# Two chunks in flight in a recurrence, and sample pages spread over a whole attention layer

## Chip, cores, metric

One Trainium2 chip, all eight cores, one launch. Each core runs the same program on its own share: a prompt of 2048 tokens and four sample sequences of four tokens. The metric is device microseconds (us) of the slowest core, from its first to its last instruction. A chip has two dies, cores 0 to 3 and cores 4 to 7.

How runs are compared needs a word, because it decides what the numbers below mean. Three things make cores differ here. (1) In some executions cores of one die run dense matmuls at a lower granted clock. (2) Even in undisturbed runs one die of a chip is slower than the other, by 25 to 90 us; on the chip of the two main profiles that is die 1, on two other chips die 0. (3) Now and then a pair of cores of the slower die is slower still. A run is labelled slow when one die is over 1% longer at a lower clock. Experiments often met a disturbed die, so I compare *medians of the four cores of one undisturbed die*: the faster die of one kernel with the faster die of another, the slower with the slower.

## Reference, cut to what matters

```python
# layer 0: eight units per token tile, four HGRN2 and four retention, each a chunked recurrence
def step(S, inp):                       # one chunk
    A = einsum(q, k) * rel              # masked decay inside the chunk
    o = einsum(A, v) + einsum(q * exp(G), S)     # inside + carried state
    S = S * exp(G_end) + einsum(k_dec, v)        # state for the next chunk
# layer 1: differential attention, 4 heads, two key maps each
#   prompt: causal softmax over 2048 tokens
#   sample: softmax over 8192 past tokens from a paged cache
k_past = cache_k[page_table]            # 64 pages of 128 tokens per sequence, in random order
v_past = cache_v[page_table]
```

Each core handles 4 x 64 = 256 pages; one page holds the keys (or values) of all four heads, 128 x 1024 elements.

## The kernel before

Every operation is put on an engine's queue by a helper, which also works out the semaphore waits: an operation waits for the last writer of what it reads, and for all readers of what it overwrites. The helper guards PSUM by bank (`P0` to `P7`). In the timeline the page work of TensorE comes in the order of the queue (transposes at 2706.68, scores at 2707.53, values at 2709.19 us on core 1, after 1.26 us of waiting, and the next prompt scores only at 2709.52), so what matters is which wait stands in front of what.

Layer 0, one unit and tile (cut): four or six projections, then the chunks one after another.

```python
def proj(ws_ap_fn, t0, n, pi, rkeys):   # pi: PSUM bank, 0, 1, 2, 0, 1, 2 ... by hand; norm in P3
    for c in range(NCH): matmul(P[pi], ...)
...
for ci in range(nchunks):
    matmul(P[4], kTt, qTt)                        # scores inside the chunk
    transpose(Pb[6], kTt); transpose(Pb[6], vTt)
    dve: Am = P[4] * mask                         # ONE Am, kvtok, qd
    act: kvtok = copy(P[6])
    matmul(P[7], kvtok_v, Am)
    matmul(P[7], Sbf, q_in)                       # carried state
    matmul(P[5], kvtok_k, kvtok_v)
    dve: U = U * decay + P[5]                     # state, float32
    dve or act: Sbf = U * ...                     # state, bf16, for the next chunk
```

Layer 1, the sample pages: a generator, one step per call, each step working on three pages.

```python
for sstep in range(NP + 2):                       # NP = 256
    stageA(sstep)       # 8 transposes of the K page into P0, copy to SBUF (DVE or ACT in turn)
    stageB(sstep - 1)   # 8 score matmuls into P1, exponential on ACT -> PTs
    stageC(sstep - 2)   # 8 value matmuls into P1 with PTs, DVE adds P1 to acc
    kdma(sstep + 2); vdma(sstep + 1)              # indirect gather of later pages
    yield
...
for h in range(4):
    load_head_weights(h); project(...)            # dense
    for each query tile, key map, key block:
        scores(kbi + 1); values(kbi)
        next(gen)                                 # one page after EVERY key block
    for each output-projection point:
        ...; next(gen)
```

## Time and profile before

The kernel took 4996.0 us (median of 20 runs on the chip of the comparison, fastest 4982.7). The phases of two cores, cut at the first matmul of each phase in the trace, in us (core 1 stands for the faster die, core 5 for the slower one):

| phase | core 1 | core 5 |
|---|---|---|
| layer 0, recurrent units | 1177 | 1171 |
| attention of heads 0, 1, 2, 3 | 382, 387, 249, 146 | 398, 400, 250, 146 |
| output projections | 117, 130, 30, 30 | 119, 129, 30, 30 |
| projections (first with the samples') | 149, 58, 57, 55 | 147, 57, 58, 55 |
| waits for the next head's weights | 31 | 35 |

The long heads are the ones with a page after each key block; all pages are used up in head 2. The prediction below shows the windows. In the profiled run cores 6 and 7 were 150 us longer than cores 4 and 5 (5124 and 5127 us against 4980 and 4971) at nearly the same clock (0.711 to 0.718). (In both main profiles every clock record is 0.5 or 1.0, half or full clock. All but the last of each core, 1302 before and 2010 after, are multiples of 3.413 us long, and on each core all begin on one grid of that step; a step of it is what the prediction sums columns over.)

### The profile page before, as it was taken

What the parts mean: (1) busy time and instruction counts of PE and PEld (TensorE: products, weight loads), DVE (VectorE), ACT (ScalarE), POOL (GpSimd) and SP (SyncE); (2) the same over time, 40 slices, a digit from 0 to 9 for tenths busy, and PEclk for the clock granted to TensorE, in tenths of its full rate; (3) what the DMA queues carried; (4) which work ended last, traced back from release to release, by engine and by line L of the source; (5) the groups of instructions that cost most, each with busy time, mean ns of one, the idle gap of its engine ahead of it and who ended that gap; (6) DMA issues with size and microseconds to landing.
All of it is one profiled execution on the core that took longest, in us unless ns stands there. A gap on an engine that the chain in (4) does not pass through costs nothing.

```text
span 5127.1 us, 60781 instructions; the slowest of 8 cores (4933.9 to 5127.1 us)
## 1 busy us (share of the span) xinstructions
PE 3005.7 (59%) x19175; PEld 1544.8 (30%) x19175; DVE 1680.8 (33%) x3705; ACT 1386.2 (27%) x2773; POOL 627.4 (12%) x712
## 2 busy tenths in 40 slices
PE   1344544555547699963645556455564565369997
PEld 1212222222222244421333333333333322124444
DVE  1235545432223344431112131211322132434445
ACT  0153333323222311133222212322213425131112
POOL 1000000011110000000133331233323100000000
PEclk9766666676668899986755557555575687679997
DMA  9700000011114011002456665566656210402201
GB/s 142 145 0 13 1 13 13 17 28 28 30 29 67 0 34 34 1 1 47 95 83 99 104 111 99 83 99 99 106 105 97 44 37 1 68 15 34 34 1 71
DMA packets 175893, 272.67 MB, mean 53 GB/s; under 512 B 14895, under 2 KB 82104, under 8 KB 175582
## 3 DMA queue, kind: packets, MB, share of 16 engines
q0 software_dynamic: 135184, 220.24, 28.0%
q1 hardware_dynamic: 40398, 48.56, 3.0%
q8 instruction: 162, 2.65, 0.2%
q14 instruction: 149, 1.22, 0.1%
HBM read 460.96 MB, written 27.98 MB: 95 GB/s over the span
## 4 chain that ended last, share of the span: by engine, by line
PE 46%; DVE 13%; issue 12%; ACT 12%; DMA 8%; another core or an unknown queue 6%; DVEq 1%; ACTq 0%; POOL 0%; SPq 0%; POOLq 0%
PE P L133 46%; ACT hT_44 L133 3%; DVE rstd_62 L133 3%; DMA wada_28_70<-w_ada 3%; DVE xT_43 L133 2%; ACT L133 2%; DMA wqkv_113<-w_in_c 2%; DVE U_93 L133 1%; DVE rb_83 L133 1%; ACT kvtok_91 L133 1%; DVE bb_82 L133 1%; ACT rstd_62 L133 1%; ACT PT_78_120 L133 1%; DVE tnrm_21_63 L133 1%
## 5 line engine op out<-in xcount | busy, mean ns | idle before, releaser
L133 DVE SCALAR_TENSOR_TENSOR xT_43<-P,modT_50,xT_43 128x4 f32<-128x4 f32 (+1 forms) x832 | 404.4, 486 | 444.3 <-PE P L133 384.3
L133 DVE TENSOR_TENSOR sqb_18_60<-P,sqb_18_60 128x257 f32<-128x257 f32 x260 | 111.0, 427 | 698.1 <-PE P L133 698.1
L133 PE MATMUL P<-sqb_18_60,ones_f_48 128*128 128x512 f32 (+1 forms) x240 | 169.6, 798 | 263.8 <-ACT sqb_18_60 L133 213.2
L133 ACT ACT_TABLE_LOAD x164 | 210.4, 1283 | 343.9 <-PE P L133 308.3
L133 DVE RECIPROCAL rstd_62<-rstd_62 128x512 f32<-128x512 f32 (+1 forms) x60 | 164.0, 2733 | 384.0 <-ACT rstd_62 L133 384.0
L133 PE MATMUL P<-Am_90,kvtok_91 64*128 64x64 bf16 (+2 forms) x224 | 47.7, 213 | 288.3 <-DVE Am_90 L133 181.8
L133 ACT COPY KTpg_89_131<-P 128x1024 bf16<-128x1024 bf16 x128 | 129.5, 1012 | 257.9 <-PE P L133 204.6
L133 PE MATMUL P<-hT_44,wqkv_113 128*128 128x512 bf16 (+1 forms) x640 | 124.1, 349 | 113.4 <-DMA wqkv_113<-w_in_c 111.1
L133 PE MATMUL P<-Vtok_117,PT_78_120 128*128 128x257 bf16 x576 | 135.8, 375 | 88.9 <-ACT PT_78_120 L133 51.2
L133 ACT COPY kvtok_91<-P 64x256 bf16<-64x256 bf16 (+3 forms) x224 | 73.7, 329 | 320.6 <-PE P L133 313.7
L133 PE MATMUL P<-QT_115,KT_116 128*128 128x512 bf16 (+1 forms) x320 | 154.6, 493 | 6.0 <-ACT stg_77_119 L133 3.8
L133 PE MATMUL P<-hT_44,wu_34_76 128*128 128x512 bf16 (+1 forms) x640 | 142.5, 378 | 22.8 <-ACT hT_44 L133 16.5
L133 PEld LDWEIGHTS P<-sqb_18_60,ones_f_48 128*128 128x128 f32 x240 | 54.7, 274 | 323.0 <-issue 321.6
L133 PE MATMUL P<-wqkv_113,hT_44 128*128 128x512 bf16 (+1 forms) x640 | 149.2, 394 | 0.6
L133 PE MATMUL P<-hT_44,wu_35_77 128*128 128x512 bf16 (+1 forms) x640 | 144.7, 382 | 8.4 <-ACT qs_79 L133 6.0
L133 DVE COPY KTpg_88_130<-P 128x1024 bf16<-128x1024 bf16 x128 | 88.5, 691 | 180.7 <-PE P L133 155.6
L133 PE MATMUL P<-qTt_84,kTt_85 128*64 128x64 bf16 (+2 forms) x224 | 54.7, 244 | 152.8 <-DVE kTt_85 L133 151.2
L133 ACT ACTIVATE rl_62_104<-P 128x512 bf16<-128x512 f32 (+1 forms) x80 | 41.1, 514 | 355.0 <-PE P L133 355.0
L133 ACT ACTIVATE rl_105_147<-P 128x512 bf16<-128x512 f32 (+1 forms) x80 | 41.1, 514 | 354.9 <-PE P L133 354.9
L133 PE MATMUL P<-identb_46,og_123 128*128 128x128 bf16 x128 | 23.8, 288 | 192.1 <-DVE small_110 L133 137.8
L133 PE MATMUL P<-hT_44,wup_99_141 128*128 128x512 bf16 (+1 forms) x640 | 120.6, 345 | 17.2 <-ACT hT_44 L133 16.5
L133 PE MATMUL P<-hT_44,wup_56_98 128*128 128x512 bf16 (+1 forms) x640 | 119.7, 343 | 17.2 <-ACT hT_44 L133 16.5
(263 smaller groups left out, 6127.4 us busy)
## 6 DMA issues: line engine op xcount, KB each, us to landing
wada_27_69<-w_ada POOLq DMA_DIRECT2D x12, 1024.0 KB, 11.5
wada_28_70<-w_ada POOLq DMA_DIRECT2D x12, 1024.0 KB, 11.3
wqkv_113<-w_in_c POOLq DMA_DIRECT2D x8, 1536.0 KB, 11.2
xld_30_72<-xp SPq DMA_DIRECT2D x8, 512.0 KB, 3.3
xld_31_73<-xp SPq DMA_DIRECT2D x8, 512.0 KB, 3.6
wu_34_76<-w_in_ab POOLq DMA_DIRECT2D x4, 1024.0 KB, 9.7
wu_35_77<-w_in_ab POOLq DMA_DIRECT2D x4, 1024.0 KB, 9.8
cosT_88<-rope SPq DMA_DIRECT2D x16, 256.0 KB, 2.7
```

The costliest lines, as they stand in the source:

```text
L133: return lambda e: getattr(e, name)(*a, **k)
```

## The change

The intent: (1) in layer 0, prepare chunk n+1 (scores, transposes, mask, copies) while the state of chunk n is on its way, so that only the state's own chain is left between chunks; (2) in layer 1, space the 258 page steps evenly over all 576 points of the layer, dense projections included, rather than putting one behind every key block until none is left.

```diff
 # layer 0
-    Am = A("Am", ...); kvtok = A("kvtok", ...); qd = A("qd", ...)
+    Am2, kvtok2, qd2 = two of each
-    def proj(ws_ap_fn, t0, n, pi, rkeys):
+    pjc = [0]
+    def proj(ws_ap_fn, t0, n, pi_unused, rkeys):
+        pi = pjc[0] % 2                       # banks P0, P1; the norm too (was P3)
+        pjc[0] += 1
-            for ci in range(nchunks):
+            def stage_x(ci):                  # scores -> P2/P3, transposes -> P4/P5, Am, kvtok, qd
+            ...
+            def stage_y(ci):                  # the three matmuls, U (P6), Sbf, output in P7
+            ...
+            stage_x(0)
+            for ci in range(nchunks):
+                if ci + 1 < nchunks:
+                    stage_x(ci + 1)
+                stage_y(ci)
 # layer 1
+    n_points = 4 * ((S // 512) * 8 + sum(4 * qt + 4 for qt in range(NQT)) * 2 + (S // 512) * 8)
+    n_steps = 4 * NPG + 2
+    def tick():
+        pace["pts"] += 1
+        want = min(n_steps, (pace["pts"] * n_steps + n_points - 1) // n_points)
+        while pace["done"] < want:
+            next(gen, None)
+            pace["done"] += 1
+    tick_hook[0] = tick                       # called after each projection tile, too
-                    for _ in range(PAGES_PER_KB):
-                        next(gen, None)
+                    tick()
```

(Cut: the bodies of the two stages, which hold the old operations in the old order, and a zeroing matmul split in three.) Eight banks are shared out anew: the double buffers take four, so projections and norm have two where they had four.

## The prediction

> **What bounds the kernel now.** I read the cores first (die 1 of the profiled run has cores in the slow state, so I use core 1 of the undisturbed die, span 4950 us), then busy time and granted clock of windows cut at the phase boundaries, then the timeline inside the phases that the change touches. Columns of the windows: length, busy us of matmul, weight load, VectorE, ScalarE and GpSimd with counts, granted clock, DMA share, GB/s.
>
> ```profile
> 351.00:985.00 634.00, 314.67 (x1549) 147.57 (x1550) 326.42 (x764) 216.91 (x350) 6.99 (x5) 0.63 0.05 10
> 985.00:1525.00 540.00, 295.85 (x1463) 134.57 (x1461) 162.34 (x310) 154.59 (x356) 86.36 (x125) 0.70 0.11 25
> 2526.00:2909.00 383.00, 222.55 (x2301) 153.91 (x2298) 95.77 (x258) 133.13 (x295) 150.15 (x161) 0.51 0.71 111
> 2909.00:3027.00 118.00, 79.23 (x833) 48.22 (x832) 48.34 (x79) 22.60 (x50) 58.23 (x62) 0.50 0.86 135
> 3042.00:3100.00 58.00, 57.73 (x257) 25.65 (x257) 9.94 (x23) 13.57 (x23) 0.00 (x0) 0.96 0.25 76
> 4025.00:4172.00 147.00, 74.02 (x388) 38.03 (x386) 32.02 (x130) 76.82 (x169) 0.00 (x0) 0.71 0.01 4
> 4172.00:4208.00 36.00, 20.55 (x64) 4.30 (x64) 24.03 (x32) 0.20 (x1) 0.71 (x1) 0.88 0.09 15
> ```
>
> Rows 1 and 2 are the HGRN and the retention units of layer 0 (the changed recurrence). Rows 3 and 4 are attention and output projection of head 0 in layer 1, with a sample page after every step; row 5 is a prompt projection (of head 1); rows 6 and 7 are attention and output projection of head 3, when no page is left. Nowhere is an engine full except TensorE in row 5: these phases are chains. Pages add 383 - 147 = 236 us for 80 pages, 2.95 us each, and the granted clock is 0.51 beside them, 0.71 without.
>
> An HGRN chunk (timeline):
>
> ```profile
> 440.97 0.35 DVE L133 SCALAR_TENSOR_TENSOR U_93<-U_93,bb_82,P 128x128 f32<-128x128 f32 x1 [0.85 <-PE P L133]
> 441.42 0.29 DVE L133 TENSOR_SCALAR Sbf_94<-U_93,bb_82 128x128 bf16<-128x128 f32 x1
> 441.62 0.21 DVE L133 TENSOR_TENSOR Am_90<-P,cf_45 64x64 bf16<-64x64 f32 x1
> 442.05 0.21 PE L133 MATMUL P<-Am_90,kvtok_91 64*128 64x64 bf16 x1 [0.79 <-DVE Am_90 L133]
> 442.19 0.24 PE L133 MATMUL P<-qTt_84,Sbf_94 128*128 128x64 bf16 x1
> 442.36 0.28 PE L133 MATMUL P<-kvtok_91 64*128 64x128 bf16 x1
> 442.75 0.35 DVE L133 SCALAR_TENSOR_TENSOR U_93<-U_93,bb_82,P 128x128 f32<-128x128 f32 x1 [0.92 <-PE P L133]
> ```
>
> U to U is 1.72 to 1.78 us: state update, Sbf, mask product Am, its matmul, the one with Sbf, the state matmul.
>
> Two page steps (TensorE timeline), of which the second begins at 2709.52:
>
> ```profile
> 2705.41 0.61 PE L133 MATMUL P<-QT_115,KT_116 128*128 128x512 bf16 x1
> 2705.82 1.07 PE L133 MATMUL P<-Vtok_117,PT_79_121 128*128 128x257 bf16 x4
> 2706.68 1.06 PE L133 MATMUL P<-identb_46,Kpg_83_125 128*128 128x128 bf16 x8
> 2707.53 0.40 PE L133 MATMUL P<-QTs_107,KTpg_88_130 128*128 128x4 bf16 x8
> 2709.19 0.39 PE L133 MATMUL P<-Vpg_87_129,PTs_91_133 128*8 128x256 bf16 x4 [1.26 <-ACT PTs_90_132 L133]
> 2709.52 0.61 PE L133 MATMUL P<-QT_115,KT_116 128*128 128x512 bf16 x1
> 2712.99 0.61 PE L133 MATMUL P<-QT_115,KT_116 128*128 128x512 bf16 x1
> ```
>
> The steps last 4.11 and 3.47 us, mean 3.79: 1.27 of prompt attention at half clock and 2.52 of page (0.85 transposes, then scores and the wait for the exponential, 1.66 where ScalarE copies the transposed page and 1.03 where VectorE does, then 0.33). TensorE's waits in layer 1's heads sum to 246 us for the page exponentials and only 28 us for K pages from DMA: the gather is hidden, and pages cost TensorE order.
>
> [...] every granted value in its clock records is 0.5 or 1.0, and nearly all lengths are multiples of 3.413 us. Summing matmul columns per such window, without transposes, over all cores: a window at half clock is followed by full clock almost never below 3000 columns, usually from 3500; one at full clock is mostly kept from about 3000. [...] page windows with some 2600 columns plus 900 of transposes stay cold. [...] page scores and page values share one bank, which is the 1.26 us wait above.
>
> **Layer 0, part by part.** HGRN: with the mask product a chunk early, U to U becomes: to Sbf 0.45, Sbf 0.29, to its matmul 0.14 (as from Am's end to its matmul elsewhere in this loop), to the state matmul 0.17, to U 0.39 = 1.44, so -0.28. Seven intervals a tile, 16 prompt tiles: -31 us. Retention: the chunk period is 2.20 us in the timeline. New: U to Sbf 0.43, Sbf on ScalarE 0.30, semaphore about 0.2, to the state matmul 0.06, to U 0.42 = 1.41; ScalarE's own work (0.30 + 0.21 + 0.44 + 0.27) fits. Three intervals, 16 tiles, 0.79: -38 us.
>
> Moved against it: projections have two PSUM banks, not three. Retention has six per tile:
>
> ```profile
> 1148.56 1.89 PE L133 MATMUL P<-hT_44,wu_35_77 128*128 128x512 bf16 x8
> 1152.46 3.52 PE L133 MATMUL P<-hT_44,wR_78 128*128 128x512 bf16 x8 [2.02 <-DVE qs_79 L133]
> 1155.77 3.71 PE L133 MATMUL P<-hT_44,wu_35_77 128*128 128x512 bf16 x16
> ```
>
> Today the third runs during the norm (1148.56) and only the fourth waits for VectorE; afterwards the third waits too, so one projection of about 1.8 us moves behind the wait: 16 tiles, +29 us. HGRN has bank readers early enough (its fifth use waits 0.3 us, hidden under scan and reciprocal). Sample chunks save the 0.15 us mask product, 32 times, and stay bound by state loads: -4. Layer 0: -31 - 38 + 29 - 4 = -44 us.
>
> **Layer 1.** Now 194 pages ride on attention of heads 0 to 2 and 64 on two output projections. Afterwards 258 steps over 576 points, one in 2.23: 57 in projections, 143 in attention, 57 in output projections.
> - Attention now: 383 + 388 + 249 + 147 = 1167 us. After: 4 x 147 = 588, plus 143 pages at 2.4 (2.52 cold, some 2.05 at full clock, since only transposes and values shrink) = 343, plus about 26 because unpaged steps, 1.0 us today in the mean of full ones, turn cold (1.28) more often: 957. Change -210.
> - Projections: +57 x 2.4 = +137; dense matmuls (1.73 us a point) keep the clock warm across a page tick.
> - Output projections now 118 + 131 + 30 + 36 = 315; after 4 x 33 + 57 x 2.5 = 275: -40, partly the K-page waits.
> - The next head's weights now always queue behind page transfers: three exposed waits of 12 to 15 us, where head 3 has none today: +10.
> Sum -103 us. The zeroing matmul split in three is nothing.
>
> **Rivals.**
> 1. Pages are simply additive. For: the page wait is inside TensorE's program order, whatever the spacing. Then 258 x 2.95 is what it was, layer 1 gains nothing, and with layer 0 and the weight wait the time is about 4960.
> 2. Pacing warms attention. Two unpaged or paged steps at half clock are 2.57 us dense and 3080 columns, about at the threshold; a gap of three points (10 in 43 pages) gives 3.85 us and reaches it in roughly half of the window phases. Once warm, a page period is 2 x 0.66 + 2.05 = 3.4 us with some 3300 columns, enough to stay. For a fully warm attention the 143 pages save 0.35 each, the 26 us fall away, and 52 full steps a head save 0.34: about -150 us more, 4700. Against: every query tile ends with a VectorE chain of several us (154 us of such waits in all), which makes it cold again, and runs are only 4 to 16 steps. I take a quarter of the time as warm.
> 3. Page ticks cool the projections (0.96 to 1.00 now): [...] a part of 228 us runs at half clock: up to +80 us, 4930.
> 4. The bank loss exceeds the retention gain: layer 0 about even, +40 us.
>
> **Range and chances.** 4996 - 44 - 103 is 4849; rival 3 weighs a little more than rival 2, so 4860. Range 4750 to 4955. More than 2% faster means below 4898, a gain of 98 us: two thirds. Within 2%: 0.31. Slower: 0.03, since it needs rivals 3 and 4 far beyond their size.
>
> **What would show it.** HGRN window (634 us) near 600, U to U near 1.45 us; retention (540) near 530, with a new idle ahead of the third projection released by VectorE's qs; heads of nearly equal length, about 385 to 410 us, where now they are some 575 with pages and 240 without; attention windows at a clock of 0.5 to 0.65; projection windows of 85 to 100 us at 0.85 or more; no waits for K pages. I am wrong if attention's clock is near 0.5 everywhere and a page still costs 2.9 us (rival 1), if projections fall to 0.7 (rival 3), or if attention's clock exceeds 0.75 (rival 2).

## More of the kernel before

One view that the prediction does not show matters later: TensorE's waits in layer 1 on core 1 (what it waited for: total us, times, longest).

```profile
PE P L133 <- ACT PTs_90_132 L133: 161.5, 128, 1.4
...
PE P L133 <- DMA Kpg_83_125<-ck,pidx_140: 11.3, 13, 1.7
```

TensorE waits in the middle of every page for its exponential (`PTs`), and hardly ever for a page from memory.

## The result, and the profile after

| | before | after |
|---|---|---|
| median of runs, us | 4996.0 (20 runs) | 4881.3 (10 runs; 4860.0 to 4925.8) |
| faster die, undisturbed | 4935 to 4951 (once 4964) | 4775 to 4793 |
| slower die, undisturbed | 4973 to 5003 (twice 5015 to 5025) | 4852 to 4864 |

The ratio is 0.9753, with a 95% interval of 0.973 to 0.9776: faster by 2.5%. (The ranges of the kernel before are from its runs beside the experiments, on three chips. Ratios here are the mean time of one kernel's fast runs over that of the other's fast runs of the same rounds, so not quite the ratio of the medians.)

The windows of core 1 after the change, which answer to those in the prediction (length, busy us of PE, PEld, DVE, ACT, POOL with counts, granted clock, DMA share, GB/s): HGRN, retention, attention of head 0, projection of head 1, attention of head 3.

```profile
351.00:954.00 603.00, 313.80 (x1541) 144.41 (x1542) 327.76 (x761) 212.84 (x343) 6.99 (x5) 0.64 0.06 10
954.00:1487.00 533.00, 307.17 (x1475) 136.91 (x1473) 166.95 (x316) 156.71 (x360) 85.47 (x125) 0.74 0.11 27
2521.00:2751.00 230.00, 116.69 (x1248) 76.59 (x1246) 59.74 (x184) 98.71 (x221) 69.43 (x74) 0.70 0.57 89
...
2824.00:2927.00 103.00, 77.34 (x609) 38.89 (x607) 22.73 (x54) 26.03 (x51) 26.55 (x29) 0.91 0.62 110
3737.00:3967.00 230.00, 116.58 (x1250) 75.66 (x1248) 59.76 (x183) 99.09 (x222) 67.83 (x73) 0.71 0.57 87
```

Head 0's attention fell from 383 us at a clock of 0.51 to 230 at 0.70, and head 3's rose from 147 to the same 230: the pages are now everywhere. The projection grew from 58 to 103 us and its clock fell from 0.96 to 0.91. Attention of head 0 on core 5, of the slower die:

```profile
2513.00:2764.00 251.00, 129.84 (x1256) 83.79 (x1256) 60.24 (x184) 98.63 (x220) 69.48 (x74) 0.64 0.53 81
```

The same instructions take 15 to 21 us longer per head there (250.8, 247.4, 243.4 and 244.4 us against 229.9, 230.9, 225.7 and 229.6), at a lower clock.

An HGRN chunk after the change (timeline of core 1):

```profile
433.89 0.35 DVE L133 SCALAR_TENSOR_TENSOR U_96<-U_96,bb_82,P 128x128 f32<-128x128 f32 x1 [0.56 <-PE P L133]
434.34 0.29 DVE L133 TENSOR_SCALAR Sbf_97<-U_96,bb_82 128x128 bf16<-128x128 f32 x1
...
434.77 0.21 PE L133 MATMUL P<-qTt_84,Sbf_97 128*128 128x64 bf16 x1 [0.43 <-DVE Am_48_90 L133]
...
435.31 0.35 DVE L133 SCALAR_TENSOR_TENSOR U_96<-U_96,bb_82,P 128x128 f32<-128x128 f32 x1 [0.56 <-PE P L133]
```

From U to U it is 1.42 us (1.71 to 1.79 before; predicted 1.44), and the chain is the predicted one: U, Sbf, its matmul, the state matmul, U. The releaser in the third row says Am, which is the last DVE operation to end before it (434.75); the matmul reads Sbf, done at 434.63, and starts 0.14 us after that, the delay that the prediction used.

The second and third projection of a retention tile (TensorE timeline of core 1):

```profile
1113.16 1.89 PE L133 MATMUL P<-hT_44,wR_78 128*128 128x512 bf16 x8
1118.78 3.51 PE L133 MATMUL P<-hT_44,wu_35_77 128*128 128x512 bf16 x8 [3.73 <-DVE qs_79 L133]
```

The third projection now waits 3.73 us for a bank, as predicted, and runs cold afterwards (3.51 us instead of 1.89). Before, the third ran under the norm and the fourth waited, 2.02 us in the tile that the prediction shows. That tile is not the common one: there the fourth ran cold (3.52), while in 10 of the 12 tiles of core 1 that follow another of the same unit it stayed warm, and the stretch of the six projections took 13.15 us where it now mostly takes 16.56.

Last, two page steps in a warm stretch of attention (TensorE timeline of core 1):

```profile
2641.39 0.61 PE L133 MATMUL P<-identb_46,Kpg_87_129 128*128 128x128 bf16 x8
...
2643.12 0.29 PE L133 MATMUL P<-Vpg_88_130,PTs_93_135 128*8 128x256 bf16 x4 [0.94 <-ACT PTs_94_136 L133]
...
2645.01 0.61 PE L133 MATMUL P<-identb_46,Kpg_85_127 128*128 128x128 bf16 x8
...
2647.11 0.29 PE L133 MATMUL P<-Vpg_89_131,PTs_94_136 128*8 128x256 bf16 x4 [1.31 <-ACT PTs_93_135 L133]
```

From one page's transposes to the next it is 3.62 us, for one page and *two* key blocks; before, a step of 3.79 us had one of each. The page still waits for its exponential (0.94 and 1.31 us): that wait was not removed.

Where the time came from, from phase lengths in the two traces, in us:

| term | predicted | core 5 | core 1 |
|---|---|---|---|
| layer 0 | -44 | -38 | -41 |
| attention | -210 | -208 | -249 |
| projections | +137 | +180 | +175 |
| output projections | -40 | -44 | -58 |
| weight waits | +10 | +3 | +3 |
| sum | -147 | -107 | -170 |

The whole spans changed by -107 (core 5, 4971 to 4864) and -167 (core 1, 4950 to 4783).

### The profile page after: what moved, and what is told of

Read it like the earlier page. It is cut to its first block, busy times and chain, and to the rows that moved or that the text cites.

```text
span 4868.4 us, 60467 instructions; the slowest of 8 cores (4766.4 to 4868.4 us)
## 1 busy us (share of the span) xinstructions
PE 2913.2 (60%) x19177; PEld 1481.6 (30%) x19177; DVE 1686.5 (35%) x3705; ACT 1380.7 (28%) x2773; POOL 626.6 (13%) x712
## 4 chain that ended last, share of the span: by engine, by line
PE 52%; DVE 13%; ACT 13%; issue 11%; DMA 9%; DVEq 1%; another core or an unknown queue 0%; ACTq 0%; SPq 0%; POOL 0%; POOLq 0%
PE P L133 52%; ACT hT_44 L133 3%; DMA wada_28_70<-w_ada 3%; DVE rstd_62 L133 3%; ACT L133 2%; DMA wqkv_116<-w_in_c 2%; DVE xT_43 L133 2%; DVE U_96 L133 1%; DVE rb_83 L133 1%; DVE bb_82 L133 1%; DMA U_96<-st_r 1%; ACT PT_81_123 L133 1%; ACT rstd_62 L133 1%; DVE tnrm_21_63 L133 1%; DVEq L121 1%
## 5 line engine op out<-in xcount | busy, mean ns | idle before, releaser
L133 PE MATMUL P<-hT_44,wqkv_116 128*128 128x512 bf16 (+1 forms) x640 | 141.8, 375 | 112.5 <-DMA wqkv_116<-w_in_c 111.4
L133 PE MATMUL P<-hT_44,wu_34_76 128*128 128x512 bf16 (+1 forms) x640 | 151.1, 388 | 56.1 <-DVE qs_79 L133 18.1
L133 PE MATMUL P<-hT_44,wu_35_77 128*128 128x512 bf16 (+1 forms) x640 | 152.7, 391 | 42.3 <-DVE qs_79 L133 21.0
L133 PE MATMUL P<-Vtok_120,PT_81_123 128*128 128x257 bf16 x576 | 124.0, 350 | 86.9 <-ACT PT_81_123 L133 55.8
L133 PE MATMUL P<-wqkv_116,hT_44 128*128 128x512 bf16 (+1 forms) x640 | 156.6, 401 | 0.6
L133 PE MATMUL P<-QT_118,KT_119 128*128 128x512 bf16 (+1 forms) x320 | 144.8, 464 | 3.2 <-ACT oTh_115 L133 2.2
L133 POOL DMA_INDIRECT Vpg_89_131<-cv,pidx_143 x85 | 79.7, 938 | 407.8 <-PE P L133 406.9
L133 PE MATMUL P<-hT_44,wup_102_144 128*128 128x512 bf16 (+1 forms) x640 | 120.5, 345 | 17.5 <-ACT hT_44 L133 16.5
L133 POOL DMA_INDIRECT Vpg_88_130<-cv,pidx_143 x86 | 80.7, 938 | 387.1 <-PE P L133 386.3
L133 PE MATMUL P<-hT_44,wup_59_101 128*128 128x512 bf16 (+1 forms) x640 | 119.2, 343 | 17.2 <-ACT hT_44 L133 16.5
```

The costliest lines, as they stand in the source:

```text
L133: return lambda e: getattr(e, name)(*a, **k)
```

## The experiments

My theory after the result: the two halves are independent; layer 0 gains by the shorter chain and pays some of it for the lost banks; layer 1 gains because spaced pages let the clock rise in attention, and pays in the projections. The rivals: the halves interact; the gain in layer 1 comes from the DMA (the gather is spread and no longer delays anything) and not from the clock; pages in the projections are a plain loss.

| label | what it is | faster die, us | slower die, us |
|---|---|---|---|
| before | | 4935 to 4951 (once 4964) | 4973 to 5003 (twice 5015 to 5025) |
| after | | 4775 to 4793 | 4852 to 4864 |
| e1_pipe | layer 0 of after, layer 1 of before | 4905 to 4914 | 4985 once, otherwise 5085 to 5108 |
| e2_pace | layer 0 of before, layer 1 of after | 4817 to 4825 | 4900 to 4904 |
| e3_banks | after, three banks for projections | 4729 to 4751 | 4850 to 4863 |
| e4_fill | after, useless matmuls added in each page | 4724 to 4729 | 4826 |
| e5_noproj | after, no pages in projections | 4797 to 4817 | 4895 and 4898, otherwise 4945 and more |
| e6_nogather_before | before, pages not gathered (wrong result) | 4834 to 4839 | 4837 to 4840 |
| e7_nogather_after | after, pages not gathered (wrong result) | 4654 to 4660 | 4655 to 4661 |
| e8_values_first | after, page values ahead of transposes | 4589 to 4620 | 4664 to 4671 |
| e9_banks_values_first | e3 and e8 together | 4540 to 4551 | 4620 to 4631 |

### e1_pipe and e2_pace: each half alone

```diff
 # e1_pipe
-layer1_mixer of the kernel after
+layer1_mixer of the kernel before
 # e2_pace
-layer0_mixer of the kernel after
+layer0_mixer of the kernel before
```

> Only the layer 0 part of the change (recurrence a chunk ahead, two projection banks); layer 1 as before. If the two parts are independent, as the prediction's sum takes them, layer 0 alone brings 38 to 44 us (0.991 to 0.993 of before, some 4955 us) and its phase lasts 1133 to 1136 us on cores 1 and 5 as after the whole change. If the parts help each other (a layer 0 that ends earlier changes nothing in layer 1, so I do not expect it), the gain would be clearly below 35 us.

> Only the pacing of the pages in layer 1; layer 0 as before. Independent parts: the rest of the gain, 123 - 41 = some 80 us on the slowest core (0.984, about 4915 us), with about 129 us on cores of die 0 and 70 us on die 1. If the pacing were worth nothing by itself (rival 1: pages are additive), 0.997 to 1.0.

Four of five runs of e1_pipe are labelled slow, so its median, 5113 us, says nothing. (In the profiled one of them this is difference (3) and not the clock: the records hold only 0.5 and 1.0, and attention of head 0 took 470 us on core 5 against 383 on core 1.) Its undisturbed die 0 lay at 4905 to 4914 us beside 4940 to 4949 of the kernel before on that die and chip: -36. Its layer 0 took 1135 us, that of the kernel after 1136. e2_pace lay at 4817 to 4825 on die 0: -122, and its attention phases took 231 to 236 us. -36 and -122 are -158, and the whole change is -160 to -167 on a faster die. The parts are independent; three quarters of the gain is the pacing. How much of the 122 us is the clock and how much the new places of the pages, these two runs do not separate.

### e3_banks: give the projections their third bank back

```diff
-        pi = pjc[0] % 2
+        pi = (0, 1, 3)[pjc[0] % 3]
-                pa, pka = P[2 + b2], f"P{2 + b2}"
+                pa, pka = P[2], "P2"
-            pns = pjc[0] % 2
+            pns = (0, 1, 3)[pjc[0] % 3]
```

> The whole change, but the masked product keeps one PSUM bank and the freed bank goes back to the projections (three in rotation). Theory that two projection banks cost 1.75 us in each of 16 retention tiles: 25 to 30 us faster than the changed kernel (about 0.969 of before, 4850 us), the retention phase some 500 us instead of 527, and the wait of the third projection for VectorE's qs product gone. Rival: the wait only moves to the next projection or the chunk loop now needs its second bank: within 8 us of the changed kernel (0.975).

The scores inside a chunk need a second bank least, since the mask product empties it at once. The window of the retention units (core 1 of this kernel):

```profile
946.00:1442.00 496.00, 299.82 (x1478) 136.78 (x1478) 167.02 (x318) 156.21 (x360) 85.50 (x125) 0.72 0.12 29
```

Retention fell from 533 to 496 us (535 to 492 on core 5), HGRN by 2 to 8; all of layer 0 from 1136 to 1091, and the faster die by some 45 us. In its TensorE timeline the third retention projection starts 1.73 us after the second again, without a wait, and takes 1.89 us.

So against the kernel after the third bank is worth 37 to 43 us in retention. This is not the prediction's term of 29 us, which counted from the kernel before. From the traces, the stretch from a retention tile's first projection to its first chunk matmul, summed over the 20 tiles, is 254 us before, 281 after and 244 in e3_banks on core 1 (252, 281 and 243 on core 5): the change lost 27 to 29 us, as predicted, and e3_banks, whose norm shares the three banks, gets more than that back. On the slower die cores 4 and 5 followed (4807 to 4849 us), but cores 6 and 7 did not (4864 to 4906): attention took 259 to 263 us per head on core 7 and 243 to 250 on cores 4 and 5, in the same program. That is difference (3); in layer 0 these two cores alone also ran 155 and 172 us at a clock of 0.8125 (see e4_fill).

### e4_fill: more work in each page step

Two matmuls of 512 columns, with results that nobody reads, go between a page's scores and its values, where TensorE waits for the exponential anyway.

```diff
+            for _ in range(2):
+                fb = next free bank of P2, P3
+                matmul(P[fb][:, 0:512], lhsT=identb, rhs=hT[:, 0, 0:512])
             for h in range(4):
                 matmul(P[1][32 * h:32 * h + 8, 64:320], lhsT=PTs..., rhs=Vpg...)
```

> The whole change plus two useless 512-column matmuls per page tick (516 in all), put into the wait for the page exponential. They add 0.21 us each of TensorE streaming at full clock, 0.43 at half clock, so 110 to 220 us of extra TensorE time, partly inside a wait of 0.6 to 1.2 us. Clock theory (a 3.41 us window needs some 3000 to 3500 columns to be followed by full clock): granted clock in the attention phases rises from 0.64 to 0.70 to over 0.85, attention gets shorter by 10 to 30 us a head, and the kernel 30 to 120 us faster than the changed one. Rival (the clock follows from the waits and is no lever; page cost is the program order on TensorE): the clock stays where it is and the kernel is 0 to 150 us slower.

If spacing helps through the clock, 512 more matmuls (two in each of 256 pages) should *shorten* the program, and if through the order or the DMA, lengthen it. Attention of head 0 on core 4 of this kernel:

```profile
2502.00:2740.00 238.00, 124.04 (x1296) 73.40 (x1318) 59.57 (x183) 98.83 (x221) 69.52 (x74) 0.77 0.57 86
```

and on the same core of the kernel after:

```profile
2520.00:2765.00 245.00, 128.15 (x1273) 83.46 (x1271) 58.88 (x179) 98.03 (x217) 70.13 (x75) 0.66 0.55 85
```

The clock rose from 0.66 to 0.77 and the phase, with more in it, became 7 us shorter (3 to 9 us over the four heads of this core). Undisturbed dies: 4724 to 4729 us against 4775 to 4793 on the faster one, 4826 against 4852 to 4864 on the slower (one run; in another, cores 6 and 7 were the longer pair again). The clock theory stands in its direction, and the kernel gained within the expected range; the expected size in attention, a clock over 0.85 and 10 to 30 us a head, was not reached. As a version it is no use: in all four runs one die ran at a lower clock and was longer, and the median was 4999 us. The trace shows what that lower clock is: on core 1 of this run the clock records hold, beside 0.5 and 1.0, a third value, 0.8125, for 1465 us, and the MLP of layer 0 took 723 us where it takes 620. The value comes by pairs of cores: on cores 0 and 1 from 243 to 3329 us, on cores 2 and 3 only from 1843 us on. Cores 4 to 7 had no such record here, though all eight run the same MLP in every run; what starts it was not shown.

### e5_noproj: no pages in the projections

```diff
-    n_points = 4 * ((S // 512) * 8 + sum(4 * qt + 4 for qt in range(NQT)) * 2 + (S // 512) * 8)
+    n_points = 4 * (sum(4 * qt + 4 for qt in range(NQT)) * 2 + (S // 512) * 8)
-    tick_hook[0] = tick
```

> The whole change, but pages are spread over attention and output projection only (258 over 448 points, one in 1.74), none in the prompt projections. In the changed kernel the projections grew by 43 to 46 us a head for 14.3 pages, 3.1 us a page, where I had put 2.4. If that term was the mis-sized one and pages in attention cost about what they cost now (2.3 to 2.7 us), moving 57 pages back would save 175 to 180 us of projection and cost 40 pages in attention and 16 in output projections at 2.6 us, 145 us: some 30 us faster than the changed kernel. Rival (clock): one page in 1.74 points leaves too few columns per window, attention falls back to a clock of some 0.55 and a page costs 2.9 us again plus cold steps: equal to the changed kernel or up to 40 us slower. The granted clock of the attention phases decides.

A page in a projection cost 3.1 us (below), so taking pages out looked like a gain. It was not: the projections fell back to 57 to 60 us, but attention grew to 260 to 273 us per head and output projections to 72 to 84, and the undisturbed, faster die lay at 4797 to 4817 us, some 27 above the kernel after. What was to decide is the clock of attention; head 0 on core 5, of the faster die:

```profile
2485.00:2745.00 260.00, 137.96 (x1491) 92.09 (x1488) 67.55 (x198) 106.66 (x237) 87.76 (x94) 0.66 0.61 97
```

It fell from about 0.70 (core 1 of the kernel after) to 0.64 to 0.66, not to the 0.55 of the rival, whose verdict (up to 40 us slower) is the one that came. All six runs are labelled slow, but the profiled one has no lowered clock on any core: its other die is the slower one of the chip, at 4895 and 4898 us in the two least disturbed runs, 31 to 46 above the kernel after. Spreading into the projections is worth its price.

### e6_nogather_before and e7_nogather_after: no page traffic

Only the first three pages are gathered, and their buffers are used for all 256 steps. The result is wrong; every instruction but the gather is the same.

```diff
-            if sstep + 2 < NP:
+            if sstep + 2 < NSL:               # NSL = 3
                 kdma(sstep + 2)
-            if sstep + 1 < NP:
+            if sstep + 1 < NSL:
                 vdma(sstep + 1)
```

> Wrong result on purpose: the kernel before, with the page gather left out after the first three pages, so that all page work runs on old buffers. If the gather is hidden, as the prediction says, only the K-page waits go: 28 us on die 0, perhaps 60 us on die 1 (its unnamed waits), nothing else. Rival (pages are bound by the gather): 150 us and more. Second question: the page exponentials start 0.3 to 0.7 us later after the scores on die 1 than on die 0; if gather traffic causes that, the dies become equal here.

> Wrong result on purpose: the changed kernel without the page gather after the first three pages. If pacing gains by clock and program order, the distance to the run before it (no gather, old schedule) stays about what it is with gather: 170 us less the K-page waits, so 130 to 160 us on die 0. Rival (pacing gains because it relieves the gather): the distance falls to the 41 us of layer 0. If gather traffic delays the page exponentials on die 1, its spans come down to those of die 0, by 60 to 80 us.

The spans by die, first of the kernel before without its gather, then of the kernel after without it:

```profile
die 0 (median of its cores): 4838.1 us, clock 0.726
die 1 (median of its cores): 4839.0 us, clock 0.728
```

```profile
die 0 (median of its cores): 4654.6 us, clock 0.785
die 1 (median of its cores): 4655.6 us, clock 0.781
```

Two things follow. First, the pacing does not gain through the DMA: without any page traffic the two kernels are still 183 us apart (31 to 42 in layer 0, the rest in layer 1), at least as much as with it. Second, my claim that the gather is hidden was wrong. It costs the kernel before some 110 us on its faster die and 150 to 160 on the slower (once 187), against the kernel before on the same chip, and the kernel after some 125 and 200. And the difference between the dies goes with the gather: without it all eight cores of either profiled run end within 22 us of each other. The long cores 6 and 7 of the first profile are explained too. Attention of head 0, core 7 of the kernel before:

```profile
2518.00:2966.00 448.00, 221.81 (x2297) 153.82 (x2296) 95.36 (x257) 134.15 (x294) 150.07 (x161) 0.51 0.62 95
```

and core 5 of the one without gather:

```profile
2527.00:2892.00 365.00, 219.47 (x2297) 155.65 (x2296) 94.92 (x257) 132.51 (x294) 1.28 (x2) 0.51 0.03 7
```

The busy times of all engines but GpSimd, which issues the gather, and the clock are nearly the same, and 83 us are gone. The wait table hid it, because on the slower die the late thing is not a page: TensorE waits for ScalarE's exponential, and this is later when pages arrive (in this window 119.8 us for the exponentials on core 7 of the kernel before, 74.3 on core 1, 66.5 without gather). On the faster die more of it stands in the table by name: of 97 us of TensorE's waits in layer 1 that are gone on core 1, 34 were for the next head's weights, 28 for K pages and 28 for exponentials. In the kernel after, the waits for exponentials in layer 1 are 273 us on core 1, 305 on core 5 and 228 on either without gather; the weights of the next head, which GpSimd issues as it does the pages, account for another 34. Why an exponential starts later beside page traffic is not settled. In the kernel before, on pages that VectorE copies, the median from last score to exponential was 0.18 us on core 1 of the faster die and 0.38 and 0.64 on cores 5 and 7 of the slower one, and no wait for a semaphore of a DMA stood there; without the gather it is 0.18 on both dies. The two runs take away the transfers and GpSimd's work of issuing them together. That work alone does not explain the difference between dies, since GpSimd is as busy on core 1 as on core 7 (150.15 and 150.07 us in attention of head 0).

The projections show what the gather does to the change. Head 1's, without gather (core 5 of e7_nogather_after):

```profile
2779.00:2872.00 93.00, 72.17 (x606) 37.51 (x604) 23.69 (x57) 26.16 (x51) 1.05 (x2) 0.94 0.16 49
```

It takes 93 us where the kernel after has 103 to 106. Summed over the heads, in the mean of the eight cores, projections go from 319 to 453 us between the two kernels without gather (+134), and from 318 to 490 (+172) between the two with it.

### e8_values_first: take the exponential's wait out of a page

```diff
         for sstep in range(NP + 2):
+            if 0 <= sstep - 2 < NP:
+                stageC(sstep - 2)
             if sstep < NP:
                 stageA(sstep)
             if 0 <= sstep - 1 < NP:
                 stageB(sstep - 1)
-            if 0 <= sstep - 2 < NP:
-                stageC(sstep - 2)
```

> The whole change with the order inside a page tick turned: values of page n-2, then transposes of page n, then scores of page n-1, so that the values no longer wait for the exponential of page n-1 on the bank that both share. Theory (a page costs TensorE order, above all the 1.0 to 1.7 us from scores to values): the tick falls by 0.6 to 1.1 us, 258 pages, 150 to 250 us faster than the changed kernel on all dies, and the wait for page exponentials (270 us on core 1) is nearly gone. Rival (the wait only moves: ScalarE's page copy and exponential then delay the prompt's exponential, and the prompt's value matmuls wait for it): under 60 us.

Values of page n-2 and scores of page n-1 share bank P1. In the old order the scores came just ahead of the values, so the values had to wait until the exponential of the *next* page had read the bank. With the values first, that exponential has the whole time between two pages. TensorE's waits in layer 1, first the kernel after (core 5, a slower die), then this one (core 1, whose die was the slower one of its chip):

```profile
PE P L133 <- ACT PTs_93_135 L133: 176.7, 108, 6.1
...
PE P L133 <- ACT PTs_94_136 L133: 127.8, 117, 4.2
```

```profile
PE P L133 <- DVE sqb L133: 153.1, 189, 3.8
...
PE P L133 <- ACT PTs L133: 18.7, 12, 4.0
```

305 us of waits for the exponential became 19, and a new, smaller one arose: the scores wait until VectorE has added the values in P1 to `acc` (stored in `sqb`). A page step (TensorE timeline of core 1):

```profile
2654.25 0.40 PE L133 MATMUL P<-Vpg,PTs 128*8 128x256 bf16 x4
...
2654.58 1.03 PE L133 MATMUL P<-identb,Kpg 128*128 128x128 bf16 x8
...
2655.76 0.59 PE L133 MATMUL P<-QT,KT 128*128 128x512 bf16 x1
```

This page takes 1.51 us from its first matmul to the next work, at half clock. It is one of the short ones: the mean of the 144 pages in attention is 2.05 us on this core, where the kernel after has 2.47 on core 1 and 2.85 on core 5. The clock of attention rose a little too, to 0.71 to 0.73. The result is correct; faster die 4589 to 4620 us, slower 4664 to 4671, so 165 to 195 below the kernel after. Ratio to the kernel before 0.9372 (0.9259 to 0.9485); the recorded verdict is unclear, with two fast runs only, one of which had die 1 at 0.8125 for some 1000 us. The medians of the undisturbed dies leave no doubt. Moving two lines gains more than the whole change, on top of which it was made; on the kernel before it was not tried.

### e9_banks_values_first: both

The edits of e3_banks and e8_values_first together.

> The changed kernel with both edits that helped by themselves: three banks for the projections and the norms of layer 0 (the masked product on one bank), and the order values(n-2), transposes(n), scores(n-1) in a page tick. If the parts are independent, as the two halves of the change were, it lies 40 to 50 us below the run with the order alone on dies in the same state: about 4560 us on a fast die, about 4620 us on the slower one, ratio to the kernel before about 0.928, layer 0's mixing about 1090 us and each head's attention 200 to 217 us. Rival (the bank gain is partly given back [...]): 10 to 25 us below only.

Faster die 4540 to 4551 us, slower 4620 to 4631: by the medians 53 and 38 below e8_values_first. The two ran on different chips, and on this one the kernel before is itself 7 and 12 us faster, which leaves about 46 and 26: as expected (40 to 50) on the faster die, at the edge of the rival's 10 to 25 on the slower one. Ratio 0.9287 (0.9198 to 0.9376), correct, the recorded verdict again unclear with two fast runs. On the faster die the two edits add up. Attention of head 0 on core 5, the faster die of that chip, takes 201 us at a clock of 0.76, where the kernel after has 230 at 0.70 on a faster die. Six of its eight runs are labelled slow (median of all 4696 us), though the profiled one of them has no lowered clock on any core; these edits do not cure the differences between dies and pairs.

## Why the prediction was right

The time was right (4881 measured, 4860 predicted, range 4750 to 4955), and so was the class. By its own steps:

- **HGRN chain**: right. U to U 1.42 us (1.44 predicted); HGRN from 627 to 602 us on core 1 and from 630 to 598 on core 5, -25 and -33 for -31. (Cut at the first matmul; the windows that the prediction named, 634 and 540 us, were cut a few us otherwise and went to 603 and 533, where it asked for about 600 and 530.)
- **Retention**: right in the sum and in both terms, one of them with luck. The net was predicted at -9 and measured at -16 and -6 (549 to 534, 541 to 535). The mean chunk period fell from 2.24 to 1.47 us, which over 44 intervals is -34 (predicted -38). (For the semaphore between ScalarE and TensorE the prediction put about 0.2 us; from the end of ScalarE's kvtok to the matmul that waited for it is 0.25 us in the retention units of core 1 before, the median of 68.) The projections of its tiles grew by 27 and 29 us (predicted 29). But the 12 prompt tiles that follow another of the same unit grew by 2.8 us each, not 1.8: the waiting projection does not only move behind the wait, it then mostly runs at half clock, 3.51 us in place of 1.89. The first tiles of the four units, 6 to 8 us shorter together, made up for it. Rival 4 (the loss exceeds the gain) did not happen.
- **Attention**: right to 2 us on the slower die, 39 too cautious on the faster. Heads were to be equal at 385 to 410 us with projection and output projection; heads 1 to 3 took 390 to 401 us on core 1 and 414 to 420 on core 5. Rival 1, plain addition, fell by the clock (0.64 to 0.71 where 0.51 was) and by e4_fill. Rival 2 came half true: I took a quarter of the time as warm and expected a clock of 0.5 to 0.65, and the 0.70 of core 1 means about 40%. Spread over the 143 pages, the excess over 588 us unpaged is 2.3 us a page on core 1 and 2.8 on core 5; I had 2.4 and a surcharge of 26 us. The prediction's limits of 3000 and 3500 columns come out of the traces of the kernel before (5 of 3115, 8 of 29, 28 of 33; see the last section); what rival 2 worked out from them was an estimate, and they do not carry over to the kernel after.
- **Projections**: the mis-sized term, +137 predicted, +175 to +180 measured. The step that failed is "+57 x 2.4 = +137": a page cost 3.1 us. What failed in it is the claim that the gather is hidden: without the gather the same term is +134, or 2.35 us a page (e6 and e7). In the trace of core 1 a page in a projection took 2.39 us from its transposes to the next work plus 0.22 ahead of them, where the exponential is waited for longest (1.69 us from scores to values, 1.31 to 1.34 in attention); without gather it took 2.0 us, nothing ahead, and 1.30 from scores to values. The clock fell as well, from 0.96 to 0.91 in head 1 (0.94 without gather), so "dense matmuls keep the clock warm across a page tick" held only nearly. So 2.4 was a good figure for a page without gather, as the sum of 2.0 and a loss of clock that the prediction did not count. That is rival 3, mild: 101 to 107 us for heads 1 to 3 where I had 85 to 100, at a clock above the 0.85 that I asked for.
- **Output projections, weight waits**: -44 and +3 on core 5 (-58 and +3 on core 1) for -40 and +10. K-page waits fell from 28 to 15 us on core 1, not to none.
- **"The gather is hidden, and pages cost TensorE order"**: wrong in its first half, right in its second. Without the gather the kernel before is 110 to 160 us faster (e6), though its table of waits has 28 us for pages. Its harm sits in the projections, where 57 pages now stand beside the gather and none did before. Attention without gather changes by -209 us in the mean of the cores (1117 to 908), where I had -210. On the slower die the gather costs the kernel after 40 to 50 us more than the kernel before, which is about what the prediction is off there (107 us for 147); that it is the whole reason is not shown. The second half is right beyond what I used it for: e8 changes only the order and gains 165 to 195 us.

What stays open: why exponentials start later beside the gather, whether by its transfers or by their issue, and why more on one die or pair of cores; which condition starts the clock of 0.8125; and what share of the pacing's gain is the clock.

## What to carry to other kernels

When a side job rides on a main loop, look first at the order inside the job: an operation that waits for something issued just before it should go first in the next round instead (165 to 195 us in e8). Spacing the job out left that wait here: 246 us for the page exponentials in layer 1 of core 1 before, 273 after. When a double buffer takes a PSUM bank from another stage, count who had that bank free at the right moment; here the cheapest bank to give up was the one that VectorE empties at once (37 to 43 us in retention, e3). And a transfer that is hardly waited for by name is not yet free (28 us of waits for pages by name on core 1, 110 to 160 us without the gather, e6): leave it out once, on purpose, and see.

## What the clock records and the gather showed

- In attention of head 0 on core 1, 88 of TensorE's 118 gaps over 0.3 us before the change and 42 of 72 after it are of 0.6 to 1.3 us; gaps of 2.4 us and more (up to 4.9 before, 5.25 after) come around the end of a query tile. The mean clock of these phases was 0.51 before and 0.64 to 0.71 after. Of the gaps over 2.3 us in layer 1's heads that began at full clock, all cores, 69 of 69 before and 99 of 110 after were at half clock 1.7 us after their end.
- The columns of a step of 3.413 us, without transposes, do not tell the next clock alone. In layer 1's heads of the kernel before, all cores, a step at half clock was followed by full clock in 5 of 3115 cases below 3000 columns, 8 of 29 from 3000 to 3500 and 28 of 33 from 3500 to 4000, and a step at full clock was kept in 20 of 120 below 3000, 12 of 13 from 3000 to 3500 and 708 of 708 above. In layer 1 of the kernel after, 171 of 452 steps at half clock with 2000 to 3000 columns were followed by full clock, and only 76 of 159 with 3000 to 4000. With two matmuls of 512 columns more in each page (e4_fill), the mean clock of attention of head 0 on core 4 was 0.77 where it was 0.66.
- The granted clock of 0.8125 (MLP 723 us for 620) came by pairs of cores: in e4_fill cores 0 and 1 from 243 us and cores 2 and 3 from 1843 us, in e8_values_first cores 6 and 7 from 318 us and cores 4 and 5 from 1384 us, in e3_banks cores 6 and 7 alone. In 8 of the 11 profiled runs no core has the value, though all eight cores run the MLP.
- Beside the page gather by indirect DMA ScalarE's small exponentials start later, without a wait for a DMA in the table, by amounts that differ between dies and pairs of cores (medians of 0.18, 0.38 and 0.64 us on cores 1, 5 and 7; 0.18 without gather). The gather as a whole is worth 110 to 200 us of 4660 to 4999 here, and the difference between the dies goes with it (4838.1 and 4839.0 us without it).
